# Loading the identity alone, halving the first token tile and the first weight block, and spreading the second gain row earlier in a hybrid encoder trunk

## The chip, the cores and the metric

The kernel runs on one core of a Trainium2 chip. The metric is the device time of one execution in microseconds, as the median of several runs. Smaller is better.

## The reference, cut to what matters

The whole program is one layer of a bidirectional encoder trunk for 512 tokens of width 1024. The change touches only its first few microseconds: the first RMSNorm, and the first product with the input projection.

```
def rmsnorm(x, g):
    y = x32 * rsqrt(mean(x32 * x32, axis=-1) + 1e-6)
    return y * g

proj = rmsnorm(x, norm_mix) @ w_in + b_in     # (512 x 1024) @ (1024 x 4624)
...                                           # two recurrent scans, out projection
x = x + cross_attention(rmsnorm(x, norm_xattn), rmsnorm(mem, norm_mem), ...)
x = x + relu(rmsnorm(x, norm_mlp) @ w_up) ** 2 @ w_down
return rmsnorm(x, norm_final)
```

## The kernel before, in words

The tokens lie in four tiles of 128 rows by 1024 columns (`xtile[0]` to `xtile[3]`, the buffers `as` in the trace). A tile is normalised, multiplied by the gain, turned by TensorE so that the columns lie on the partitions, and split into a high part (fp32r, made by ScalarE) and a low part (the rest, made by VectorE). The weights come in blocks of 128 by 1024 (`st`) that are split in the same way into `wh` and `wl` (`split_out`, L258). A product is then three matmuls: high times high, high times low and low times high (`mm3`, L261 to L263).

The gain row must stand on all 128 partitions. It arrives as one row of 4 KB (`grow1[96:97]`, the buffer `rg`, L149) and TensorE spreads it, 512 columns at a time, by a product with a matrix of ones into PSUM (`spread(0)` and `spread(1)`, L164; the results are `gmix[0]` and `gmix[1]`). `keep_busy` (L160) issues matmuls whose result nobody reads. The constants `cs` (L151) hold the identity that the transposes need (`ident`), two masks and a small selector, 392 columns in all.

For tile 0 the order is written out by hand for TensorE, VectorE and ScalarE, and each of these engines works through its own queue in that order:

- `x_stat(0)`: the sum of squares, half of it on ScalarE (L333), half on VectorE (L335), the two added on VectorE (L336); then GpSimd takes the power -0.5 (L340).
- `x_scale(0, 0)` (L344, VectorE): the left 512 columns times that number and times `gmix[0]`.
- `x_turn(0, 0)` (L349, TensorE): four transposes of 128 columns. Then `spread(1)`.
- `split(0)`: weight block 0 into high and low; `x_split(0, 0)`: the transposes' result into high and low.
- `x_stat(1)` (L338, ScalarE): the sum of squares of tile 1, behind tile 0's split in ScalarE's queue. GpSimd's power, VectorE's `x_scale(1, 0)` and the split of weight block 1 follow it.
- `part_v(0, 0)`: the first six matmuls of the product, tile 0 with weight block 0. Then the transposes of tile 1 and `part_v(0, 1)`, tile 0 with weight block 1, and so on.

The loads go through two queues. SP's queue issues tile 0, weight block 0, tile 1, weight block 1, tiles 2 and 3, and further weight blocks. ScalarE's queue issues the gain row and behind it `cs`.

Of the kernel before, what the change touches and what calls it, by code (L numbers as in the profile page):

```python
# [11 lines left out]
F32R = mybir.dt.float32r  # L12
U8 = mybir.dt.uint8
AF = mybir.ActivationFunctionType
ALU = mybir.AluOpType
# [3 lines left out]
P = 128  # L19
# [20 lines left out]
C_ID, C_MF, C_MB, C_SEL, NC1 = 0, 128, 256, 384, 392  # L40
# [40 lines left out]
def trunk(ctx: ExitStack, tc: tile.TileContext, x, mem, wpk, vec, cst, lmask, rmask, rows, out):  # L81
    nc = tc.nc
# [4 lines left out]
    v, sc, gp, pe = nc.vector, nc.scalar, nc.gpsimd, nc.tensor  # L87
    cnt = [0]

    def nm(s):  # L90
        cnt[0] += 1
        return f"{s}_{cnt[0]}"

    def T(tag, w, bufs, dt=F32):
        return (sb if w == 516 else big).tile([P, w], dt, tag=tag, name=nm(tag), bufs=bufs)

    def mmb():
        return psm.tile([P, 512], F32, tag="mm", name=nm("mm"))

    def smb():  # L100
        return pss.tile([P, 512], F32, tag="sm", name=nm("sm"))

    def tiny(w):
        return sb.tile([P, w], F32, tag=f"tiny{w}", name=nm("tiny"), bufs=2 if w == 8 else 6)

    def ap(t, off, *dims):
        a = t[:, :]
        return bass.AP(a.tensor, a.offset + off, [list(a.ap[0])] + [list(d) for d in dims])
# [12 lines left out]
    cs = sb.tile([P, NC1], F32, name="cs")  # L121
# [3 lines left out]
    ident = cs[:, C_ID:C_ID + P]  # L125
    grow1 = RG()
# [3 lines left out]
    xtile = [z[:, 0:1024] for z in xfull]  # L130
# [10 lines left out]
    def behind(a, b):  # L141

        tc.add_manual_dep(a.ins, b.ins.name, mybir.DependencyInfo(mybir.DependencyClass.NoSync, mybir.DependencyReason.DATA),
                          reason="order of an engine")

    def load_x(t):
        nc.sync.dma_start(out=xtile[t], in_=x[t * P:t * P + P, :])

    row_load = nc.scalar.dma_start(out=grow1[96:97, :], in_=rows[0:1, :])  # L149
    load_x(0)  # L150
    behind(nc.scalar.dma_start(out=cs, in_=cst[:, 0:NC1]), row_load)  # L151
    for g in range(2):
        v.memset(grow1[0:96, g * 512:g * 512 + 512], 0.0)
    gmix = [smb(), smb()]
    idle = mmb()

    def keep_busy(n):

        for _ in range(n):
            pe.matmul(idle[:, 0:P], lhsT=ones[:, 0:P], rhs=ones[:, 0:P], start=True, stop=True)  # L160

    def spread(g):

        pe.matmul(gmix[g], lhsT=ones[0:97, 0:P], rhs=grow1[0:97, g * 512:g * 512 + 512], start=True, stop=True)  # L164

    with tc.manual_schedule(engines={mybir.EngineType.PE}):
        keep_busy(6)
        spread(0)
        keep_busy(4)

    def small_setup():
        lmf = A4()
        nc.sync.dma_start(out=vc, in_=vec)
        nc.sync.dma_start(out=lmf[:, 0:len(LEVELS) * P], in_=lmask)
        for j in range(2):
            a = lmf[64 * j:64 * j + 64, 64 * j:NLV * P]
            v.tensor_copy(lm[64 * j:64 * j + 64, :].rearrange("p (l t) -> p l t", t=64),
                          bass.AP(a.tensor, a.offset, [list(a.ap[0]), [P, NLV], [1, 64]]))
        le, lr = tiny(8), tiny(8)
        lg = vc[:, V_LB:V_LB + 8]  # L180
        v.tensor_tensor(out=le, in0=lg, in1=lg, op=ALU.subtract)
        sc.activation(le, le, AF.Exp)
        v.reciprocal(lr, le)
        v.tensor_tensor(out=le, in0=le, in1=lr, op=ALU.mult)
        v.tensor_tensor(out=lb[:, 0:8], in0=le, in1=le, op=ALU.subtract)
        v.tensor_scalar(out=lb[:, 8:16], in0=lb[:, 0:8], scalar1=-1.0, scalar2=1.0, op0=ALU.mult, op1=ALU.add)
        v.tensor_copy(selr[0:64, :], cs[0:64, C_SEL:C_SEL + 8])
        v.tensor_copy(selr[64:128, :], cs[0:64, C_SEL:C_SEL + 8])
        v.tensor_scalar(out=negb, in0=vc[:, V_FF:V_FF + 8], scalar1=-1.0, scalar2=None, op0=ALU.mult)
# [40 lines left out]
    st_tiles, hl_tiles = {}, {}  # L230

    def load(i):
        if i >= NSTREAM or i in st_tiles:
            return
        t = T("st", 1024, 3)
        nc.sync.dma_start(out=t, in_=wpk[i])
        st_tiles[i] = t

    def split(i):
        if i >= NSTREAM or i in hl_tiles:  # L240
            return
        load(i)
        s = st_tiles[i]
        hi, lo = T("wh", 1024, 3, F32R), T("wl", 1024, 3, F32R)
        made = split_out(hi, lo, s)
        hl_tiles[i] = (hi, lo)
        return made[1]
# [9 lines left out]
    def split_out(dst_hi, dst_lo, src):  # L257
        return sc.activation(dst_hi, src, AF.Copy), v.tensor_tensor(out=dst_lo, in0=src, in1=dst_hi.bitcast(F32), op=ALU.subtract)  # L258
# [56 lines left out]
    xT = XT()  # L315
# [10 lines left out]
    rx, tp = {}, {}  # L326

    def x_stat(t):

        ss = tiny(1)  # L330
        if t == 0:
            s0, s1 = tiny(1), tiny(1)
            sc.activation(junk[:, 512:1025], xfull[t][:, 512:1025], AF.Square, scale=1.0 / 32, accum_out=s1)  # L333
            xg = xfull[t][:, 0:512]
            v.scalar_tensor_tensor(out=junk0[:, 0:512], in0=xg, scalar=1.0 / D, in1=xg, op0=ALU.mult, op1=ALU.mult, accum_out=s0)  # L335
            v.tensor_tensor(out=ss, in0=s0, in1=s1, op=ALU.add)  # L336
        else:
            sc.activation(junk, xfull[t], AF.Square, scale=1.0 / 32, accum_out=ss)  # L338
        rx[t] = tiny(1)
        gp.tensor_tensor(out=rx[t], in0=ss, in1=nh, op=ALU.pow)  # L340

    def x_scale(t, g):
        xg = xtile[t][:, g * 512:g * 512 + 512]
        v.scalar_tensor_tensor(out=xg, in0=xg, scalar=rx[t], in1=gmix[g], op0=ALU.mult, op1=ALU.mult)  # L344

    def x_turn(t, g):
        tp[t, g] = smb()
        for k in range(4):
            pe.transpose(tp[t, g][:, k * P:k * P + P], xtile[t][:, g * 512 + k * P:g * 512 + k * P + P], ident)  # L349

    def x_split(t, g):
        p3 = tp[t, g][:, :].rearrange("p (k t) -> p k t", t=P)
        split_out(ap(xT[g], t * P, [1024, 4], [1, P]), ap(xT[g], 512 + t * P, [1024, 4], [1, P]), p3)

    acc_v = [mmb() for _ in range(4)]

    def part_v(t, q):
        w = hl_tiles[q]  # L360
        for k in range(2):
            kk = 2 * q + k
            z = slice(k * 512, k * 512 + 512)
            mm3(acc_v[t], xs[kk][0][:, t * P:t * P + P], xs[kk][1][:, t * P:t * P + P], w[0][:, z], w[1][:, z], kk == 0, kk == 7)

    ET = mybir.EngineType
    with tc.high_priority(), tc.manual_schedule(engines={ET.PE, ET.DVE, ET.Activation}):
        x_stat(0)
        x_scale(0, 0)
        x_turn(0, 0)  # L370
        spread(1)
        split(0)
        x_split(0, 0)
        x_stat(1)
        part_v(0, 0)
        x_scale(1, 0)
        x_turn(1, 0)
        split(1)
        x_stat(2)
        part_v(0, 1)  # L380
        x_split(1, 0)
        x_scale(2, 0)
        part_v(1, 0)
        x_turn(2, 0)
        x_stat(3)
        x_scale(3, 0)
        part_v(1, 1)
        x_turn(3, 0)
        x_scale(0, 1)
        x_split(2, 0)  # L390
        x_scale(1, 1)
        part_v(2, 0)
        x_split(3, 0)
        x_turn(0, 1)
        split(2)
        part_v(2, 1)
        x_split(0, 1)
        x_turn(1, 1)
        x_scale(2, 1)
        part_v(3, 0)  # L400
        x_split(1, 1)
        x_scale(3, 1)
        part_v(3, 1)
        x_turn(2, 1)
        x_split(2, 1)
        part_v(0, 2)
        x_turn(3, 1)
        x_split(3, 1)
        part_v(1, 2)
        part_v(2, 2)  # L410
        split(3)
        part_v(3, 2)
        small_setup()


# [484 lines left out]
    for t in range(2):  # L900
        a = mt[t]
# [5 lines left out]
        ss = tiny(1)  # L907
# [418 lines left out]
    for f in range(4):  # L1326
# [6 lines left out]
        for p in range(4):  # L1333
            a = []
# [14 lines left out]
            h, l = a11[:, o:o + 256], a11[:, o + 256:o + 512]  # L1349
# [6 lines left out]
            s1, s2, s3, s4 = sa[:, 0:256], sa[:, 256:512], sb_[:, 0:256], sb_[:, 256:512]  # L1356
# [106 lines left out]
```

## Time and profile before

| what | value |
|---|---|
| median of 3 runs | 832.44 us (832.35 to 832.47) |
| time of the profiled execution | 832.41 us |
| its span, first to last instruction | 830.3 us |
| mean granted TensorE clock | 0.998 |
| busy: PE, DVE, ACT, POOL | 818.2, 594.5, 430.0, 77.4 us |

PE is TensorE's matmuls, PEld its weight loads, DVE is VectorE, ACT is ScalarE, POOL is GpSimd, SP is SyncE; ACTq and SPq are the queues from which DMAs are issued. The time lies 2.1 us above the span. PE is busy for nearly the whole span, so what a change in the first microseconds is worth shows as a shift of everything behind it.

### The profile page before, as it was taken

Reading aid. Unit: us, or ns where it says so; the run is one execution under the profiler, and the core shown is the slowest. Engines: PE = TensorE matmul, PEld = TensorE weight load, DVE = VectorE, ACT = ScalarE, POOL = GpSimd, SP = SyncE. Lnnn points to the kernel's source line nnn. Section 1 sums busy time; section 2 is a strip of 40 time slices with the busy share of each in tenths; the row PEclk is TensorE's granted clock in tenths of the full one; section 3 lists DMA queues with packets and bytes.
Section 4 is the critical chain, followed back from the end, with each engine's and each line's share of the span. In section 5 each row is a group of like instructions: output and inputs, shape, how many; then the busy total and the mean of one; then the engine's idle time right before and its main releaser. Section 6 shows DMA issues by size and latency. Waiting matters only on the chain.

```text
span 830.3 us, 11722 instructions
## 1 busy us (share of the span) xinstructions
PE 818.2 (99%) x4414; PEld 681.7 (82%) x4414; DVE 594.5 (72%) x1046; ACT 430.0 (52%) x767; POOL 77.4 (9%) x131
## 2 busy tenths in 40 slices
PE   8999999999999999999999999999999999999996
PEld 6788888887878989887888888888888888888885
DVE  6568875699569988555558985676568666756685
ACT  5247455443678475455546575453444345434544
POOL 2000000100010000100000004012102210220001
PEclk9999999999999999999999999999999999999999
DMA  7332223222342344532352349969836982798332
GB/s 276 117 133 78 77 78 102 79 89 79 117 123 68 123 138 147 151 98 85 118 127 60 84 124 299 264 158 270 238 102 176 274 214 98 185 293 206 109 69 102
DMA packets 34122, 118.86 MB, mean 143 GB/s; under 512 B 3921, under 2 KB 4049, under 8 KB 34066
## 3 DMA queue, kind: packets, MB, share of 16 engines
q1 hardware_dynamic: 22832, 77.80, 27.4%
q0 software_dynamic: 10944, 39.85, 21.7%
q8 instruction: 35, 0.57, 0.3%
q10 hardware_dynamic: 290, 0.47, 0.2%
q14 instruction: 21, 0.17, 0.1%
HBM read 116.00 MB, written 2.10 MB: 142 GB/s over the span
## 4 chain that ended last, share of the span: by engine, by line
PE 89%; issue 5%; DVE 2%; DMA 1%; ACT 1%; POOL 1%; POOLq 0%; ACTq 0%
PE mm L261 18%; PE mm L263 18%; PE mm L262 18%; PE sm L1155 6%; PE sm L1153 6%; PE sm L1154 6%; PE sm L485 2%; PE mm L1155 2%; PE mm L1153 2%; PE mm L1154 2%; PE sm L827 1%; PE sm L562 1%; DVE wl L258 1%; PE sm L263 1%; PE sm L261 1%
## 5 line engine op out<-in xcount | busy, mean ns | idle before, releaser
L258 ACT ACTIVATE wh<-st 128x1024 fp32r<-128x1024 f32 x131 | 138.7, 1060 | 189.8 <-PE mm L262 117.8
L261 PE MATMUL mm<-xT,wh 128*128 128x512 f32 x544 | 215.2, 396 | 0.0
L258 DVE TENSOR_TENSOR wl<-st,wh 128x1024 fp32r<-128x1024 f32 x131 | 160.2, 1224 | 75.5 <-ACT wh L258 75.0
L263 PE MATMUL mm<-xT,wl 128*128 128x512 f32 x544 | 213.0, 392 | 0.1
L262 PE MATMUL mm<-xT,wh 128*128 128x512 f32 x544 | 212.3, 390 | 0.3 <-DVE xT L975 0.3
L263 PEld LDWEIGHTS mm<-xT,wl 128*128 128x128 f32 x544 | 102.1, 188 | 21.7 <-DVE wl L258 0.3
L262 PEld LDWEIGHTS mm<-xT,wh 128*128 128x128 f32 x544 | 102.2, 188 | 21.0 <-DVE xT L975 0.9
L261 PEld LDWEIGHTS mm<-xT,wh 128*128 128x128 f32 x544 | 102.2, 188 | 20.9 <-ACT wh L258 0.3
L1102 POOL DMA_DIRECT2D as<-in_wpk x52 | 39.6, 764 | 250.2 <-DVE wl L258 165.1
L1342 DVE SCALAR_TENSOR_TENSOR t<-mm,rg 128x512 f32<-128x512 f32 x32 | 22.0, 691 | 52.1 <-PE mm L263 52.0
L1153 PE MATMUL sm<-wh,yT 128*128 128x512 f32 x128 | 49.8, 389 | 0.0
L1154 PE MATMUL sm<-wl,yT 128*128 128x512 f32 x128 | 49.8, 389 | 0.0
L1155 PE MATMUL sm<-wh,yT 128*128 128x512 f32 x128 | 49.8, 389 | 0.0
L258 ACT ACTIVATE wh<-as 128x1024 fp32r<-128x1024 f32 x26 | 27.6, 1062 | 37.0 <-PE sm L1155 23.7
L258 DVE TENSOR_TENSOR wl<-as,wh 128x1024 fp32r<-128x1024 f32 x26 | 31.9, 1226 | 14.0 <-ACT wh L258 13.9
L1153 PE MATMUL sm<-wh,a 128*128 128x512 f32 x84 | 32.9, 391 | 0.0
L1155 PE MATMUL sm<-wh,a 128*128 128x512 f32 x84 | 32.7, 389 | 0.0
L1154 PE MATMUL sm<-wl,a 128*128 128x512 f32 x84 | 32.7, 389 | 0.0
L1285 DVE TENSOR_TENSOR vv<-vv,sm 128x512 f32<-128x512 f32 x48 | 31.0, 681 | 1.7 <-PE sm L1155 1.7
L199 POOL TENSOR_TENSOR tiny<-tiny,misc 128x4 f32<-128x4 f32 (+1 forms) x10 | 9.6, 963 | 204.6 <-DVE tiny L197 139.5
L1154 PEld LDWEIGHTS sm<-wl,yT 128*128 128x128 f32 x128 | 24.0, 188 | 5.0
L1155 PEld LDWEIGHTS sm<-wh,yT 128*128 128x128 f32 x128 | 24.0, 188 | 5.0
(329 smaller groups left out, 1581.1 us busy)
## 6 DMA issues: line engine op xcount, KB each, us to landing
st<-in_wpk SPq DMA_DIRECT2D x131, 512.0 KB, 3.4
as<-in_wpk POOLq DMA_DIRECT2D x52, 512.0 KB, 7.0
gate<-in_wpk POOLq DMA_DIRECT2D x24, 512.0 KB, 6.9
as<-in_x SPq DMA_DIRECT2D x4, 512.0 KB, 6.7
vv<-in_x SPq DMA_DIRECT2D x8, 256.0 KB, 4.5
out<-vv SPq DMA_DIRECT2D x7, 256.0 KB, 2.2
a<-in_mem SPq DMA_DIRECT2D x2, 512.0 KB, 3.7
t<-in_rows SPq DMA_DIRECT2D x2, 256.0 KB, 4.9
```

What stands on the lines that cost most here:

```text
L199: gp.tensor_tensor(out=r, in0=ms, in1=nh.to_broadcast([P, w]), op=ALU.pow)
L258: return sc.activation(dst_hi, src, AF.Copy), v.tensor_tensor(out=dst_lo, in0=src, in1=dst_hi.bitcast(F32), op=ALU.subtract)
L261: pe.matmul(ps, lhsT=ah, rhs=bh, start=first, stop=False)
L262: pe.matmul(ps, lhsT=ah, rhs=bl, start=False, stop=False)
L263: pe.matmul(ps, lhsT=al, rhs=bh, start=False, stop=last)
L485: mm = pe.matmul(ps[64 * i:64 * i + 64, z:z + 64], lhsT=kc[j][:, w * P + 64 * i:w * P + 64 * i + 64], rhs=rhs(j, w * P, i), start=True, st ...
L1102: return gp.dma_start(out=dst, in_=wpk[idx], **kw)
L1153: pe.matmul(ps, lhsT=ah, rhs=bh, start=new, stop=False, **fl)
L1154: pe.matmul(ps, lhsT=ah, rhs=bl, start=False, stop=False, **fl)
L1155: pe.matmul(ps, lhsT=al, rhs=bh, start=False, stop=end and k == 1, **fl)
L1285: added = v.tensor_tensor(out=z, in0=z, in1=ps, op=ALU.add if sign > 0 else ALU.subtract)
L1342: v.scalar_tensor_tensor(out=y, in0=ps, scalar=0.0, in1=rrow[:, 0:512], op0=ALU.max, op1=ALU.mult)
```

## The change

Five edits, all for the first tile:

1. ScalarE's queue loads the identity first (128 columns instead of the 392 of `cs`) and the gain row behind it. The other 264 columns of `cs` are loaded later by SP's queue, between `vc` and the level masks.
2. `spread(1)` stands directly behind `spread(0)`, ahead of the transposes. Of the four `keep_busy` matmuls behind `spread(0)` one is left.
3. The two halves of tile 0's sum of squares are added by GpSimd instead of VectorE.
4. `x_scale(0, 0)`, `x_turn(0, 0)` and `x_split(0, 0)` are each cut into two pieces of 256 columns (`first_half`, `first_split`).
5. The split of weight block 0 is cut into two pieces of 512 columns (`weight_half`); on each of ScalarE and VectorE the order is weight half 0, tile half 0, weight half 1, tile half 1.

```diff
-    row_load = nc.scalar.dma_start(out=grow1[96:97, :], in_=rows[0:1, :])
+    id_load = nc.scalar.dma_start(out=ident, in_=cst[:, C_ID:C_ID + P])
     load_x(0)
-    behind(nc.scalar.dma_start(out=cs, in_=cst[:, 0:NC1]), row_load)
+    behind(nc.scalar.dma_start(out=grow1[96:97, :], in_=rows[0:1, :]), id_load)
...
         keep_busy(6)
         spread(0)
-        keep_busy(4)
+        spread(1)
+        keep_busy(1)
...
         nc.sync.dma_start(out=vc, in_=vec)
+        nc.sync.dma_start(out=cs[:, P:NC1], in_=cst[:, P:NC1])
...
-            v.tensor_tensor(out=ss, in0=s0, in1=s1, op=ALU.add)
+            gp.tensor_tensor(out=ss, in0=s0, in1=s1, op=ALU.add)
...
+    def first_half(h):
+        z = slice(h * 256, h * 256 + 256)
+        a = xtile[0][:, z]
+        v.scalar_tensor_tensor(out=a, in0=a, scalar=rx[0], in1=gmix[0][:, z], op0=ALU.mult, op1=ALU.mult)
+        tp[h] = smb()
+        for k in range(2):
+            pe.transpose(tp[h][:, k * P:k * P + P], xtile[0][:, h * 256 + k * P:h * 256 + k * P + P], ident)
+
+    def first_split(h):
+        p3 = tp[h][:, 0:256].rearrange("p (k t) -> p k t", t=P)
+        split_out(ap(xT[0], h * 2048, [1024, 2], [1, P]), ap(xT[0], h * 2048 + 512, [1024, 2], [1, P]), p3)
+
+    def weight_half(h):
+        z = slice(h * 512, h * 512 + 512)
+        split_out(hl_tiles[0][0][:, z], hl_tiles[0][1][:, z], st_tiles[0][:, z])
...
+        hl_tiles[0] = T("wh", 1024, 3, F32R), T("wl", 1024, 3, F32R)
         x_stat(0)
-        x_scale(0, 0)
-        x_turn(0, 0)
-        spread(1)
-        split(0)
-        x_split(0, 0)
+        first_half(0)
+        first_half(1)
+        weight_half(0)
+        first_split(0)
+        weight_half(1)
+        first_split(1)
         x_stat(1)
```

On ScalarE the queue began like this before (`rg` is the gain row, `cs` the constants, `as_71` tiles 0 and 1, `wh` and `xT` the high parts of weights and tokens, the last row tile 1's sum of squares):

```order
L149 DMA rg_70<-in_rows 1x1024
L139 ACT_TABLE_LOAD
L139 ACTIVATE misc<-misc 128x1
L151 DMA cs<-in_cst 128x392
L333 ACTIVATE xT_106,tiny_127<-as_71 128x513
L258 ACTIVATE wh_140<-st_107 128x1024
L258 ACTIVATE xT_105<-sm_134 128x4x128
L338 ACTIVATE xT_106,tiny_146<-as_71 128x1025
```

Now ScalarE's queue begins like this:

```order
L149 DMA cs<-in_cst 128x128
L139 ACT_TABLE_LOAD
L139 ACTIVATE misc<-misc 128x1
L151 DMA rg_70<-in_rows 1x1024
L335 ACTIVATE xT_104,tiny_127<-as_71 128x513
L260 ACTIVATE wh_123<-st_105 128x512
L260 ACTIVATE xT_103<-sm_134 128x2x128
L260 ACTIVATE wh_123<-st_105 128x512
L260 ACTIVATE xT_103<-sm_138 128x2x128
L340 ACTIVATE xT_104,tiny_149<-as_71 128x1025
```

The gain row has moved from the first to the second place among the DMAs, and half of the weight block's split from ahead of tile 0's split to its middle.

On TensorE the start of the program was this before (L160 is `keep_busy`, L164 `spread`, L349 the transposes, L261 and on the product):

```order
L160 MATMUL mm_89<-t_4_74 128x128 x6
L164 MATMUL sm_87<-rg_70,t_4_74 128x512
L160 MATMUL mm_89<-t_4_74 128x128 x4
L349 MATMUL sm_134<-cs,as_71 128x128 x4
L164 MATMUL sm_88<-rg_70,t_4_74 128x512
L261 MATMUL mm_119<-wh_140,xT_105 128x512
```

It is now this (L366 is the transposes in `first_half`, L263 the product's first matmul):

```order
L160 MATMUL mm_89<-t_4_74 128x128 x6
L164 MATMUL sm_87<-rg_70,t_4_74 128x512
L164 MATMUL sm_88<-rg_70,t_4_74 128x512
L160 MATMUL mm_89<-t_4_74 128x128
L366 MATMUL sm_134<-cs,as_71 128x128 x2
L366 MATMUL sm_138<-cs,as_71 128x128 x2
L263 MATMUL mm_117<-wh_123,xT_103 128x512
```

The second spread has moved from behind the transposes to ahead of them, so everything on TensorE from the transposes on now stands behind both spreads.

## Rows read from the trace of the kernel before

**Rows 1.** Stretches of 20 us: busy time of each engine, granted clock, DMA
```profile
0.00:20.00 20.00, 17.18 (x81) 13.07 (x82) 12.64 (x19) 11.37 (x18) 4.46 (x21) 1.00 0.75 286
20.00:40.00 20.00, 19.91 (x95) 15.85 (x94) 11.25 (x24) 5.54 (x8) 0.00 (x0) 1.00 0.39 121
```
**Rows 2.** Chain of work, first 12 us: start, duration, what
```profile
1.36 5.42 DMA cs<-in_cst
...
9.29 0.57 POOL tiny L340
...
10.54 1.23 DVE wl L258
11.81 0.50 PE mm L262
```
**Rows 3.** Timeline of TensorE: start, duration, operation, count [idle before]
```profile
1.00 2.93 PE L160 MATMUL mm<-t 128*128 128x128 f32 x12 [1.00 <-POOL as L138]
3.72 1.26 PE L164 MATMUL sm<-rg,t 97*128 97x512 f32 x2
4.82 1.06 PE L160 MATMUL mm<-t 128*128 128x128 f32 x8
6.91 0.63 PE L349 MATMUL sm<-cs,as 128*128 128x128 f32 x4 [1.04 <-DMA cs<-in_cst]
7.38 1.02 PE L164 MATMUL sm<-rg,t 97*128 97x512 f32 x2
```
**Rows 4.** Timeline of ScalarE, 4 to 9 us
```profile
4.42 0.63 ACT L333 ACTIVATE xT<-as 128x513 fp32r<-128x513 f32 x1 [1.62 <-DMA as<-in_x]
4.95 0.19 ACT L333 ACTIVATION_READ_ACCUMULATOR xT<-as 128x1 f32 x1
5.82 1.06 ACT L258 ACTIVATE wh<-st 128x1024 fp32r<-128x1024 f32 x1 [0.68 <-DMA st<-in_wpk]
7.58 0.60 ACT L258 ACTIVATE xT<-sm 128x512 fp32r<-128x512 f32 x1 [0.70 <-PE sm L349]
8.07 1.05 ACT L338 ACTIVATE xT<-as 128x1025 fp32r<-128x1025 f32 x1
```
**Rows 5.** Timeline of VectorE and GpSimd, 5 to 9 us
```profile
5.17 0.16 DVE L336 TENSOR_TENSOR tiny<-tiny,tiny 128x1 f32<-128x1 f32 x1
5.41 0.55 POOL L340 TENSOR_TENSOR tiny<-tiny,misc 128x1 f32<-128x1 f32 x1 [4.30 <-DVE tiny L336]
6.00 0.75 DVE L344 SCALAR_TENSOR_TENSOR as<-as,tiny,sm 128x512 f32<-128x512 f32 x1 [0.67 <-POOL tiny L340]
6.91 1.23 DVE L258 TENSOR_TENSOR wl<-st,wh 128x1024 fp32r<-128x1024 f32 x1 [0.16 <-ACT wh L258]
8.21 0.69 DVE L258 TENSOR_TENSOR xT<-sm,xT 128x512 fp32r<-128x512 f32 x1
```
**Rows 6.** DMA issues: ScalarE's first (ACTq), SP's second (SPq), its time to landing
```profile
0.74 0.53 ACTq L149 DMA_DIRECT2D rg<-in_rows  x1
1.17 0.42 SPq L236 DMA_DIRECT2D st<-in_wpk  x1
st<-in_wpk SPq DMA_DIRECT2D x1, 512.0 KB, 4.6
```
**Rows 7.** DMA queues, stretches from 1.6, 2.0 and 4.2: packets, MB, share
```profile
q10 hardware_dynamic: 2, 0.00, 3.1%
...
q1 hardware_dynamic: 194, 0.73, 95.7%
...
q1 hardware_dynamic: 204, 0.76, 79.1%
q10 hardware_dynamic: 144, 0.20, 23.1%
```
**Rows 8.** DMA packets from 14.75 to 15.0 us, mostly of 468 bytes
```profile
DMA packets 78, 0.08 MB, mean 325 GB/s; under 512 B 64, under 2 KB 64, under 8 KB 78
q1 hardware_dynamic: 78, 0.08, 95.0%
```

## The prediction

> **What bounds the kernel now.** [...]
>
> Next the chain of waits [rows 2], to see what the start waits for. It runs from the constants' DMA (1.36 to 6.78) through the transposes, then ScalarE's sum of squares of tile 1 (8.07, [rows 4]), GpSimd's power (9.29), `x_scale(1, 0)` and the low part of weight block 1 on VectorE (10.54 to 11.77) to the matmul at 11.81. From there on TensorE is fed. **So the time that counts is not the first product of tile 0, but when ScalarE begins tile 1's sum of squares: 8.07.** Tile 0's product begins in the shadow of that chain. In ScalarE's queue that sum stands behind all of tile 0's split, and its row shows no wait of its own: tile 1 had landed.
>
> Last the timelines of tile 0 [rows 3 to 5]. The transposes at 6.91 waited for the constants, which landed at 6.78, but the scaling that they also need ran from 6.00 to 6.75. The two arrive almost together; an earlier identity alone would give 0.1 us.
>
> **The change part by part.** The sum is made for the start of tile 1's sum of squares.
>
> *Gain row behind the identity.* This is the costly edit. Before, the row was ScalarE's first DMA, issued at 0.74 [rows 6], and its two packets moved before 2.0 (the first stretch, 1.6 to 2.0) [rows 7]. Now it takes the place of `cs`, issued at about 1.36 [rows 2]. How was a DMA served that was issued there? From 2.0 to 4.2 the queue q10, which is ScalarE's, moved no packet at all, and SP's q1 moved 194; all 144 of `cs` moved between 4.2 and 6.6 [rows 7]. Weight block 0, issued by SP at 1.17, landed at 1.17 + 4.6 = 5.77 [rows 6], in the middle of that. So the constants were served as if all DMAs stood in one line by time of issue: behind tile 0 and weight block 0. The row is a single data packet on one engine, so its turn comes anywhere in that stretch; I take the middle, 5.4, and the bounds 4.7 (first packets at 4.2, plus the identity's 0.2 below, plus 0.3 for the packet and its signal) and 6.3 (block 0's landing at 5.77 plus the same).
>
> Both spreads wait for it. The spread at 7.38 took 1.02 for two records of 0.59 that start 0.43 apart; its weights lead by about 0.2 [rows 3]. With the row at 5.4, `spread(0)` ends at 5.4 + 0.2 + 1.02 = 6.62.
>
> *`spread(1)` ahead of the transposes.* Two more records (2 x 0.43) and one `keep_busy` (two passes of 1.06 / 8 = 0.13 each) stand ahead of the transposes: 5.4 + 0.2 + 4 x 0.43 + 0.26 = 7.58 instead of 6.91. Before, the second spread cost nothing: it ran from 7.38 to 8.40 while ScalarE split tile 0 from 7.58 [rows 3, 4]. Now its cover is gone.
>
> *Scaling in halves.* A half costs 0.48: 0.75 less a slope of (1.23 - 0.69) / 512 per column times 256 [rows 5]; the bounds are half of 0.75 and all of it. 6.64 to 7.6 for both halves: hidden, since TensorE is free only at 7.58. The transposes end for half 0 at 7.97 (two of the four, some 0.39 of 0.63), for half 1 at 8.21.
>
> *ScalarE's queue.* Its weight half 0 is done early. From the transposes on, one after another: tile half 0, 0.37; weight half 1, 0.60; tile half 1, 0.37. (The 1024 columns took 1.06 and the 512 took 0.60, so 256 less are 0.23 less; an instruction starts some 0.1 before the end of the one ahead, as 8.07 against 7.58 + 0.60 [rows 4].) That is 8.01 to 8.38, to 8.88, to 9.15, and tile 1's sum begins at 9.05. Before, ScalarE did the whole weight block from 5.82 to 6.88, while it had to wait for the transposes anyway, and only one instruction of 0.60 stood between transposes and sum. **Cutting the weight block moves 0.5 us of ScalarE's work from that free time onto the path.**
>
> *Sum: 9.05 - 8.07 = +1.0 us.* The power, `x_scale(1, 0)` and block 1's low part follow unchanged, 12.8 instead of 11.81, and TensorE's feed begins 1.0 later.
>
> *The add on GpSimd.* VectorE's add took 0.16 [rows 5]. No plain add of GpSimd stands in the trace; the bounds are 0.16 and its power on the same shape, 0.55. I take 0.35, 0.2 more than before. It is hidden behind the gain row: the power ends by 6.4 at most with tile 0 0.2 later, and `spread(0)` at 6.62. If the row came early, it would show in full. [...]
>
> *Identity first.* 128 packets of 512 bytes, 8 on each of 16 engines. Small packets took about 0.02 each: 95% of 16 engines in 0.25 us is 3.8 us, less 14 large ones of 0.17 (33.7 us of engine time by 194 in [rows 7]), by 64 [rows 8]. So 0.2 us, which tile 0 may lose if the identity goes first: 0 to 0.2. Later loads gain some 0.4 (`cs` took 23.1% of 16 x 2.4 us, 0.55 an engine [rows 7]), but tile 1 wasn't waited for: no gain. The other 264 columns come behind `vc`, long before the copy into `selr`: nothing.
>
> The profiled execution took 832.41, almost the median of 832.44; so 833.4.
>
> **Rivals.**
>
> *The row comes in time: 832.8.* If the queues take turns, the row follows the identity on its own queue and needn't wait for weight block 0; it lands by 4.5 and both spreads end before the scaling. What speaks for it: the row has only one packet, and was issued within 0.2 us of block 0. Against it: q10's silence from 2.0 to 4.2 [rows 7]. Then the power sets the path. Tile 0 at 4.42 to 4.6, ScalarE's half of the sum done 0.72 later (5.14 to 5.32 [rows 4]), add and hops 0.25 to 0.65, power 0.55: 5.96 to 6.5. First half scaled 0.5 later, its two transposes 0.45, then ScalarE's 0.37 + 0.60 with the overlaps, and the sum of tile 1 begins 1.1 behind the transposes: 8.0 to 8.55, which is -0.1 to +0.5 us, middle +0.35. So even with the row in time there is no gain to speak of, since the halved weight block sits in ScalarE's queue. [...]
>
> *Slow passes at the start: 835, slower.* The first 12 passes of `keep_busy` took 2.93 / 12 = 0.24 each, the eight from 4.82 only 0.13 [rows 3], although the granted clock is given as 1.00 [rows 1]. The pace changed while TensorE was working without a break. Now it has nothing to do from 3.93 until the row lands. If the pace rises late for that, the four spread records start 0.85 apart instead of 0.43, +1.7 us, and the passes of `keep_busy` and the transposes add 0.2: +2.9 in all, 835.3. For it: a pause of 1.5 us where there was none. Against it: nearly all of the work before the change of pace remains. It decides from 1.66 us on (below); in the likeliest case, without it, the row would have to land after 6.05.
>
> *Faster.* It would need tile 1's sum to start before 8.07; all low bounds together give 0.1 us. The work taken away (three `keep_busy`, 0.8 us) lies where TensorE waits.
>
> **How the numbers follow.** The row late at the normal pace 0.52 (+0.3 to +1.9, since every 0.1 of the row's landing is 0.1 of the end), the row in time 0.30, slow passes 0.15, something faster 0.03. The forecast is the likeliest, 833.4. The range 832.3 to 834.7 takes in the second case and the first; it leaves out most of the slow passes and the faster case, under 0.2. A measurement of this kernel can tell about 0.2%, 1.66 us, from no change. The late row beyond 6.05 (0.05) and most of the slow passes (0.13) are slower by that: 0.18; faster 0.03; the same 0.79.
>
> **What the profile will show.** The gain row's DMA lands between 4.7 and 6.3; `spread(0)` begins right behind it, and VectorE's first scaling waits for TensorE, not for GpSimd. The transposes begin at about 7.6, ScalarE's sum of tile 1 at about 9.05, and the last matmul that waits for weight block 1 at about 12.8. Wrong it would be if spreads ran before 5 (the row in time), if their records started more than 0.5 apart (slow passes), or if TensorE's long feed began before 11.8 (a gain that I don't see). If the start is late but the end isn't, some wait behind 12 us had slack that the chain doesn't show.

## The result, and the profile after

The changed kernel takes **835.13 us** in the median of seven runs (833.33 to 836.49), the kernel before 832.44 (832.33 to 832.59, seven runs); the ratio is 1.0032, with an interval of 1.0022 to 1.0042. It is slower, by more than the 0.2% that can be told from no change, and outside the forecast range.

The seven runs fall into two groups by their span: one of 831.0 us and six of 833.0 to 833.3, with no run between. The profiled execution is the one short run, 833.33 us. So this section shows what the change does in the shorter runs; what the longer ones add is shown by the first experiment.

The timeline of TensorE in the changed kernel, to be read against [rows 3]:

```profile
0.99 2.93 PE L160 MATMUL mm<-t 128*128 128x128 f32 x12 [0.99 <-POOL as L138]
4.91 1.96 PE L164 MATMUL sm<-rg,t 97*128 97x512 f32 x4 [0.99 <-DMA rg<-in_rows]
6.70 0.39 PE L160 MATMUL mm<-t 128*128 128x128 f32 x2
6.93 0.83 PE L366 MATMUL sm<-cs,as 128*128 128x128 f32 x4
...
11.13 0.63 PE L351 MATMUL sm<-cs,as 128*128 128x128 f32 x4 [1.31 <-issue]
...
12.22 0.50 PE L264 MATMUL mm<-wl,xT 128*128 128x512 f32 x1 [0.23 <-DVE wl L260]
```

TensorE now stands idle for 0.99 us until the gain row has landed, and runs both spreads (four records, at the usual 0.43 us from one to the next, the first 0.50). The transposes begin at 6.93, where they began at 6.91 before. The matmul that waits for weight block 1 begins at 12.22 instead of 11.81.

ScalarE's timeline in the changed kernel [rows 4]:

```profile
4.73 0.63 ACT L335 ACTIVATE xT<-as 128x513 fp32r<-128x513 f32 x1 [2.05 <-DMA as<-in_x]
...
7.40 0.38 ACT L260 ACTIVATE xT<-sm 128x256 fp32r<-128x256 f32 x1 [0.83 <-PE sm L366]
7.68 0.62 ACT L260 ACTIVATE wh<-st 128x512 fp32r<-128x512 f32 x1
8.20 0.38 ACT L260 ACTIVATE xT<-sm 128x256 fp32r<-128x256 f32 x1
8.46 1.06 ACT L340 ACTIVATE xT<-as 128x1025 fp32r<-128x1025 f32 x1
```

From the first transposed half on, three instructions stand ahead of tile 1's sum of squares, 7.40 to 8.46, 1.06 us; before it was one, 7.58 to 8.07. The sum begins 0.39 later than before.

GpSimd's and VectorE's part [rows 5]:

```profile
5.54 0.19 POOL L338 TENSOR_TENSOR tiny<-tiny,tiny 128x1 f32<-128x1 f32 x1 [4.43 <-ACT xT L335]
5.80 0.55 POOL L342 TENSOR_TENSOR tiny<-tiny,misc 128x1 f32<-128x1 f32 x1
```
```profile
6.39 0.87 DVE L363 SCALAR_TENSOR_TENSOR as<-as,tiny,sm 128x256 f32<-128x256 f32 x2 [1.02 <-POOL tiny L342]
```

VectorE's scaling waits for GpSimd's power here, not for the spread.

The chain of waits, as far as it has the rows that answer to [rows 2], and the DMA queues of the stretch from 2.0 to 4.2 us [rows 7]:

```profile
0.74 0.41 ACTq L149
...
1.25 3.53 DMA rg<-in_rows
...
4.91 1.96 PE sm L164 x4
...
8.58 1.04 ACT xT L340 x2
...
9.69 0.56 POOL tiny L342
...
10.94 1.23 DVE wl L260
```

```profile
q1 hardware_dynamic: 141, 0.52, 62.1%
q10 hardware_dynamic: 139, 0.07, 14.7%
```

The gain row has taken the constants' place at the head of the chain: issued at 1.25, landed at 4.78. The identity's packets now move on q10 in a stretch in which q10 was silent before, and the row's one packet of 4 KB moves behind most of them, at 4.09.

In the short run the wait at 12.22 is 0.41 late and the span is 0.6 longer (830.95 against 830.33). VectorE's last instruction is 0.35 late (826.11 for 825.76); the other 0.27 lies behind it. In the nine profiles with the constants in two loads 4.83 to 4.85 us follow that instruction, in the five with one load 4.55 to 4.57. At the end SP waits for the semaphores of the DMAs one after another; with one DMA more, ScalarE's last store, which was waited for last before (by 829.43), is now waited for first (until 829.62), and all other waits come behind it.

Six runs of seven have 2 us more than that.

### The profile page after: what moved, and what is told of

It is laid out like the page before. It is cut to its first block, busy times and chain, and to the rows that moved or that the text cites. A ratio compares the mean times of both kernels' runs of the same rounds, so it can differ in the third digit from the quotient of the medians.

```text
span 831.0 us, 11715 instructions
## 1 busy us (share of the span) xinstructions
PE 817.7 (98%) x4408; PEld 681.2 (82%) x4408; DVE 594.3 (72%) x1048; ACT 429.8 (52%) x769; POOL 77.8 (9%) x132
## 4 chain that ended last, share of the span: by engine, by line
PE 89%; issue 5%; DVE 2%; ACT 1%; DMA 1%; POOL 1%; POOLq 0%; ACTq 0%
PE mm L263 18%; PE mm L265 18%; PE mm L264 18%; PE sm L1178 6%; PE sm L1177 6%; PE sm L1176 6%; PE sm L508 2%; PE mm L1177 2%; PE mm L1178 2%; PE mm L1176 2%; PE sm L850 1%; PE sm L585 1%; DVE wl L260 1%; PE sm L265 1%; PE sm L264 1%
## 5 line engine op out<-in xcount | busy, mean ns | idle before, releaser
L260 ACT ACTIVATE wh<-st 128x1024 fp32r<-128x1024 f32 (+1 forms) x132 | 138.9, 1053 | 189.8 <-PE mm L264 117.5
L263 PE MATMUL mm<-xT,wh 128*128 128x512 f32 x544 | 215.3, 396 | 0.0
L260 DVE TENSOR_TENSOR wl<-st,wh 128x1024 fp32r<-128x1024 f32 (+1 forms) x132 | 160.2, 1215 | 75.6 <-ACT wh L260 75.0
L263 PEld LDWEIGHTS mm<-xT,wh 128*128 128x128 f32 x544 | 102.2, 188 | 21.0 <-ACT wh L260 0.3
```

Source lines behind the costliest of these rows:

```text
L263: pe.matmul(ps, lhsT=ah, rhs=bh, start=first, stop=False)
```

## The experiments

**What was to be told apart.** Theory A: in the longer runs the row lands as in the short one, but TensorE's passes are still at the slow pace of the first 12 `keep_busy` passes when the spreads run, so that the four records start 0.85 us apart. Theory B: it is the loads, the gain row or another of the start landing some 2 us later in the longer runs.

**The changed kernel again**, without an edit, for a profile of a longer run.

> The changed kernel, not altered, for more times and a second profile. Its first profile is the fastest of seven runs (833.33; span 831.0, the others about 833.1). Theory A (slow passes): TensorE's pause between the first keep_busy matmuls and the gain row lets the first stretch run at the slow pace in most runs. Then there are two groups of spans, about 831.0 and about 833.1, nothing between, and a profile of the slow group has the four spread records about 0.85 us apart instead of 0.43, the transposes near 9 us and the end 2 us later. Theory B (late row): the gain row lands later in most runs than the 4.78 us of the first profile, up to 6.3. Then spans are spread without gaps, and a slow profile has records 0.43 apart that begin near 6.5 us.

Measured: 835.44 us median (832.96 to 836.57, seven runs), ratio 1.0028 (1.0017 to 1.004). Four spans lie at 833.2 to 833.5, three at 830.9 to 831.3. The profiled execution has 833.4. The timelines of TensorE, VectorE and ScalarE, and of the windows view the row of 6 to 8 us (busy time of PE, PEld, DVE, ACT and POOL, then granted clock, DMA share and GB/s):

```profile
4.99 3.75 PE L164 MATMUL sm<-rg,t 97*128 97x512 f32 x4 [1.07 <-DMA rg<-in_rows]
8.53 0.64 PE L160 MATMUL mm<-t 128*128 128x128 f32 x2
8.96 0.90 PE L366 MATMUL sm<-cs,as 128*128 128x128 f32 x4
...
14.45 0.50 PE L264 MATMUL mm<-wl,xT 128*128 128x512 f32 x1 [0.23 <-DVE wl L260]
```
```profile
7.14 0.87 DVE L363 SCALAR_TENSOR_TENSOR as<-as,tiny,sm 128x256 f32<-128x256 f32 x2 [1.68 <-PE sm L164]
```
```profile
10.69 1.06 ACT L340 ACTIVATE xT<-as 128x1025 fp32r<-128x1025 f32 x1
```
```profile
6.00:8.00 2.00, 2.00 (x4) 0.97 (x3) 0.85 (x3) 0.63 (x1) 0.46 (x1) 1.00 1.03 420
```

Theory A holds, B falls. The spreads begin at 4.99, 0.08 after those of the short run, so the row landed as it did there, and tile 0 and weight block 0 are no more than 0.15 later. But the four records take 3.75 us instead of 1.96, and every row behind them is 2.0 to 2.2 late: the transposes at 8.96 (6.93), tile 1's sum at 10.69 (8.46), the last wait at 14.45 (12.22).

The granted clock reads 1.00 in that stretch, as in the short run, but that figure is no measurement there. The trace records the clock only from its first change on, and the view counts the time before as 1.00. The first record, a rise to 1.00, stands at 9.56 us in this run and at 3.92 in the short one, and at 4.19 in the kernel before; in each of the three TensorE's passes and transposes start 0.21 apart before that moment and 0.11 apart after it. So the 1.00 of [rows 1] says nothing of the first 4.19 us either.

**Three more `keep_busy` ahead of the spreads**, so that TensorE doesn't stand idle while the row is on its way.

```diff
-        keep_busy(6)
+        keep_busy(9)
         spread(0)
```

> The changed kernel with nine keep_busy matmuls instead of six ahead of the first spread, so that TensorE works without a break until about the row's landing at 4.8 us. Nothing else is changed, the row still comes second. Theory A: the slow group goes, all runs lie near 833.3 (832.41 + 0.7 to 1.0) and within 0.5 us of each other. Theory B: as slow and as spread as the changed kernel, about 835.

Measured: 833.80 us (833.17 to 835.04, 11 runs), ratio 1.0014 (1.0006 to 1.0023). Nine spans lie at 831.1 to 832.0, so the runs don't agree within the 0.5 us that theory A expected. The group at 833 with a mean granted clock of 0.997 or more is gone, though the row lands as before (the spreads begin at 5.00). Two runs are longer, with spans of 832.9 and 833.2, and in those two the mean granted clock is 0.995. The profiled execution is one of them: TensorE's timeline, and the windows of 12 to 14 and 14 to 16 us:

```profile
5.00 2.22 PE L164 MATMUL sm<-rg,t 97*128 97x512 f32 x4
...
7.28 0.60 PE L366 MATMUL sm<-cs,as 128*128 128x128 f32 x4
...
11.42 0.63 PE L351 MATMUL sm<-cs,as 128*128 128x128 f32 x4 [1.32 <-issue]
...
12.51 0.80 PE L264 MATMUL mm<-wl,xT 128*128 128x512 f32 x1 [0.23 <-DVE wl L260]
13.10 0.63 PE L265 MATMUL mm<-wh,xT 128*128 128x512 f32 x1
13.53 0.63 PE L263 MATMUL mm<-wh,xT 128*128 128x512 f32 x1
```
```profile
12.00:14.00 2.00, 1.77 (x6) 1.20 (x5) 1.74 (x3) 1.63 (x3) 1.00 (x2) 0.61 1.04 358
14.00:16.00 2.00, 2.00 (x7) 1.58 (x6) 1.47 (x3) 0.00 (x0) 1.93 (x8) 0.54 0.95 309
```

This is another loss, at another place: after TensorE had nothing to do for 1.3 us ahead of tile 1's transposes, the granted clock reads 0.61 and 0.54 over these 4 us, and seven matmuls start up to 0.43 apart instead of 0.23: some 1.5 us, about as much as this run is longer than the kernel's short ones (832.9 against 831.1 to 831.4). The runs of the changed kernel have 0.997 to 0.999, so this loss is not theirs. The clock's first rise stands at 5.62 here, during the spreads.

**The same, and four `keep_busy` ahead of tile 1's transposes.**

```diff
+        keep_busy(4)
         x_scale(1, 0)
         x_turn(1, 0)
```

> The changed kernel with nine keep_busy matmuls ahead of the first spread and four more between tile 0's first product and tile 1's transposes, where TensorE otherwise pauses for 1.3 us. The granted clock fell to 0.5 behind that pause in one run with nine. Theory A with the fall: no run shows a granted clock under 1 from 12 to 16 us, the group at 834.8 to 835.0 goes, all runs 833.2 to 833.9. If the fall has nothing to do with the pause, some runs stay near 835.

Measured: 833.34 us (832.80 to 833.96, 11 runs), ratio 1.001 (1.0001 to 1.0019); spans 830.9 to 832.1 in one group, granted clock 0.997 to 0.999 in every run. TensorE's timeline:

```profile
5.00 2.65 PE L164 MATMUL sm<-rg,t 97*128 97x512 f32 x4
...
10.39 1.05 PE L160 MATMUL mm<-t 128*128 128x128 f32 x8
11.86 0.63 PE L351 MATMUL sm<-cs,as 128*128 128x128 f32 x4 [0.42 <-issue]
```

With both pauses filled both kinds of longer run are gone. In this run the four records took 2.65: here too the clock rose only during the spreads, at 6.54, but earlier than the 9.56 of the long run. What is left, 1.0 us against the kernel before, is the late row, ScalarE's order, the 0.27 at the end and, in the profiled run, 0.7 us of slow passes.

**The gain row first, the identity second**, in the changed kernel: no pause at all ahead of the spreads.

```diff
-    id_load = nc.scalar.dma_start(out=ident, in_=cst[:, C_ID:C_ID + P])
+    row_load = nc.scalar.dma_start(out=grow1[96:97, :], in_=rows[0:1, :])
     load_x(0)
-    behind(nc.scalar.dma_start(out=grow1[96:97, :], in_=rows[0:1, :]), id_load)
+    behind(nc.scalar.dma_start(out=ident, in_=cst[:, C_ID:C_ID + P]), row_load)
```

> The changed kernel with the two DMAs of ScalarE's queue exchanged: gain row first, identity second. TensorE then goes from keep_busy to the spreads without a break. Theory A and theory B both expect the time back near before: the power on GpSimd sets the path, tile 1's sum of squares begins near 8.3 us, 832.5 to 832.9, no slow group. If the cost lies in the halves, in GpSimd's add or in the second spread's new place instead (theory C), it stays at 833.3 or above.

Measured: 833.44 us (832.65 to 834.38, 11 runs), ratio 1.0012 (1.0003 to 1.0021); eight spans at 830.8 to 831.5, three at 832.3 to 832.5, those three with a mean granted clock of 0.995. TensorE's timeline of a short run (span 831.3):

```profile
3.72 3.51 PE L164 MATMUL sm<-rg,t 97*128 97x512 f32 x4
...
12.52 0.50 PE L264 MATMUL mm<-wl,xT 128*128 128x512 f32 x1 [0.23 <-DVE wl L260]
```

Theories A and B both expected 832.5 to 832.9; the median lies above, at what theory C expected (833.3 or more). The profile corrects theory A in one point. There is no pause ahead of the spreads here, and yet the four records take 3.51 us, from 3.72 to 7.23; the first clock record, the rise, stands at 6.98. So no pause is needed for slow passes: the pace is slow from the start until the clock rises (passes 0.21 apart, then 0.11), and when that is differs from run to run, from 3.92 to 9.56 in the profiles up to here. The pause still matters. Without one ahead of the spreads the clock had risen by 6.98 in the profiles of three kernels (5.62, 6.54, 6.98), and none of their 33 runs lies with the longer group but for a later fall (the longest without one 832.1); the 9.56 was seen only with the pause. Why a pause should do that, no run here shows.

**Edit 1's order alone**, in the kernel before: identity first, row second, the rest of `cs` later; everything else as before.

```diff
-    behind(nc.scalar.dma_start(out=cs, in_=cst[:, 0:NC1]), row_load)
+    behind(nc.scalar.dma_start(out=grow1[96:97, :], in_=rows[0:1, :]), id_load)
```

> The kernel before with the DMA edit alone: identity first, gain row second, the rest of the constants later; spreads, halves and add as before. Theory A: TensorE has the same pause, so two groups again; at the normal pace about 832.6, at the slow pace the scaling waits for two slow spread records, some 0.8 to 1.2 us more, 833.5 to 834. Theory B: one group, 832.6 to 834 without gaps. Theory C: no change, 832.4.

Measured: 834.49 us (832.58 to 834.59, 11 runs), ratio 1.0018 (1.0009 to 1.0027). Two groups again: three spans at 830.6 to 831.0 and eight at 832.0 to 832.6, whose times (834.00 to 834.59) lie above the 833.5 to 834 expected. The profile shows a short run:

```profile
4.86 1.10 PE L164 MATMUL sm<-rg,t 97*128 97x512 f32 x2 [0.93 <-DMA rg<-in_rows]
5.79 1.06 PE L160 MATMUL mm<-t 128*128 128x128 f32 x8
...
11.91 0.50 PE L263 MATMUL mm<-wl,xT 128*128 128x512 f32 x1 [0.25 <-DVE wl L259]
```

Edit 1 alone gives the longer runs, with only one spread ahead of the transposes: 0.1 us up to the last wait in the profiled short run (11.91 for 11.81), some 2 us in a long one (832.0 to 832.6 for 830.3). The four `keep_busy` are eight passes, and like the spread they stand between the row and the transposes. That no long run was profiled here leaves the slow passes in it argued from the first experiment.

**Edit 2's order alone**, in the kernel before: `spread(1)` behind `spread(0)`, one `keep_busy` instead of four, the row still loaded first.

> The kernel before with edit 2 alone: second spread directly behind the first, one keep_busy matmul behind them, gain row first as before. There is no pause. If the second spread's place costs only where the passes are still slow (the profile of the changed kernel with the row first had four slow records from 3.72 to 7.2), the transposes stand at 6.9 to 7.4 by the run: 832.4 to 832.9, hardly above before. If its place alone costs 2 us, 834.5.

Measured: 832.77 us (832.21 to 834.01, 11 runs), ratio 1.0006 (0.9997 to 1.0015), all spans at 830.2 to 830.8. TensorE's timeline:

```profile
3.71 2.34 PE L164 MATMUL sm<-rg,t 97*128 97x512 f32 x4
5.90 0.39 PE L160 MATMUL mm<-t 128*128 128x128 f32 x2
6.99 0.63 PE L350 MATMUL sm<-cs,as 128*128 128x128 f32 x4 [0.71 <-DMA cs<-in_cst]
```

With the row first, the spreads and the passes behind them end 0.71 us before the transposes, which wait for the constants, although the first two records were slow (2.34 us for the four). Slow passes have that much room here, and 1.04 us in the kernel before [rows 3].

**`spread(1)` behind the transposes**, in the changed kernel, and then **the same with the row first**.

```diff
         spread(0)
-        spread(1)
         keep_busy(1)
...
         first_half(1)
+        spread(1)
         weight_half(0)
```

> The changed kernel with the second spread put back behind the transposes, all else (gain row second, pause, halves, GpSimd's add) as in the change. Theory A (slow passes, and the second spread's place lets them count): at the slow pace two records of 0.85 us fewer stand ahead of the transposes, so the slow group comes from +2.5 down to about +0.7 us, median 833.0 to 833.4. Theory B (the row's landing alone) expects only the two records at the normal pace, 0.86 less, 834.3.

> The changed kernel with the gain row first and the second spread behind the transposes. Nothing slow stands ahead of the transposes any more but the first spread, as before. Theory A: 832.5 to 832.9, one group; what stays above before is the halved weight block in ScalarE's queue and the later tile 0, tile 1's sum of squares at about 8.3. If TensorE's later pause of 1.3 us (10.1 to 11.4) makes the granted clock fall in some runs, those lie 1.6 above.

Measured: 833.84 us (832.84 to 835.32, 11 runs), ratio 1.0017 (1.0008 to 1.0025), with spans from 830.9 to 832.8; and with the row first 832.74 us (832.58 to 833.86, 11 runs), ratio 1.0006 (0.9997 to 1.0015), spans 830.7 to 831.5. Putting the second spread back takes 1.3 us off the median, putting the row back as well the rest of what can be measured. The first of the two medians lies between what theory A (833.0 to 833.4) and theory B (834.3) expected, so it doesn't decide between them.

The profile with the row second (a shorter run, span 830.9) shows which clock the slow pace goes with: the second spread on TensorE's timeline, and the window of 8 to 10 us.

```profile
7.67 1.91 PE L164 MATMUL sm<-rg,t 97*128 97x512 f32 x2
```
```profile
8.00:10.00 2.00, 2.00 (x4) 0.87 (x4) 1.18 (x3) 2.00 (x5) 0.40 (x1) 0.50 1.04 424
```

Behind pauses of 0.89 and 0.70 us the granted clock has fallen to 0.50, and this is recorded. The spread's two records start 0.85 apart, as in the first experiment's long run. The fall made this run no longer: three others without it (mean clock 0.998 for 0.995) have spans of 831.0.

**Edits 4 and 5 alone**, the halves of tile 0 and of weight block 0, in the kernel before.

```diff
...
-        x_scale(0, 0)
-        x_turn(0, 0)
+        first_half(0)
+        first_half(1)
         spread(1)
-        split(0)
-        x_split(0, 0)
+        weight_half(0)
+        first_split(0)
+        weight_half(1)
+        first_split(1)
```

> The kernel before with edits 4 and 5 alone: scaling, transposes and split of tile 0 and the split of weight block 0 in halves; DMAs, spreads and add as before. By the prediction's count tile 1's sum of squares begins 0.2 to 0.5 us later, for half of the weight block sits in ScalarE's queue behind the transposes: 832.6 to 832.9. If the halves let the first product start earlier and that counted, below 832.3.

Measured: 833.00 us (832.61 to 833.30, 11 runs), ratio 1.0008 (0.9999 to 1.0016), spans 830.6 to 831.2. ScalarE's timeline:

```profile
7.47 0.38 ACT L258 ACTIVATE xT<-sm 128x256 fp32r<-128x256 f32 x1 [0.80 <-PE sm L364]
7.75 0.62 ACT L258 ACTIVATE wh<-st 128x512 fp32r<-128x512 f32 x1
8.27 0.38 ACT L258 ACTIVATE xT<-sm 128x256 fp32r<-128x256 f32 x1
8.53 1.06 ACT L338 ACTIVATE xT<-as 128x1025 fp32r<-128x1025 f32 x1
```

Tile 1's sum begins at 8.53, 0.46 late, with no other edit: the same three instructions as in the changed kernel. Of the 0.46, 0.11 is the transposes' own delay in this run (7.02 for 6.91, behind the constants); 0.35 is the halves. The median lies a little above the 832.6 to 832.9 expected, and the interval can't tell it from before.

**Edit 3 alone**, the add on GpSimd, in the kernel before.

> The kernel before with edit 3 alone, the add on GpSimd. The profile of the changed kernel shows the add at 0.19 us and the power 0.34 behind the end of ScalarE's half of the sum, where before it was 0.27. So 0.1 us, hidden in part behind the constants' landing: 832.35 to 832.5, not to be told from before. If GpSimd's add held up more than that, 832.7 or above.

Measured: 832.47 us (832.24 to 833.07, 11 runs), ratio 1.0002 (0.9993 to 1.0011): no difference that can be measured.

**What the parts suggest as a faster kernel**: the row first, the identity alone second, tile 0 in halves, weight block 0 split whole and ahead of their splits, `spread(1)` behind the transposes, four `keep_busy`, the add on VectorE.

> A version that keeps what costs nothing: gain row first, identity alone second, scaling, transposes and split of tile 0 in halves; but the weight block split whole ahead of the tile, the second spread behind the transposes, four keep_busy matmuls behind the first spread and the add on VectorE. ScalarE's tile halves follow the transposes at about 6.95 and 7.4, tile 1's sum of squares begins at about 7.7 instead of 8.07: 832.0, faster than before by 0.3 to 0.5 us. If the sum's start isn't what sets the path, 832.4.

Measured: 832.26 us (832.12 to 833.03, 11 runs) against 832.35, ratio 0.9999 (0.999 to 1.0008). ScalarE's timeline:

```profile
7.01 0.78 ACT L259 ACTIVATE xT<-sm 128x256 fp32r<-128x256 f32 x2 [0.29 <-PE sm L365]
7.94 1.07 ACT L339 ACTIVATE xT<-as 128x1025 fp32r<-128x1025 f32 x1 [0.15 <-DMA as<-in_x]
```

Tile 0's split is done 0.4 us earlier than before, but tile 1's sum gains only 0.13: it now waits for tile 1's own load. VectorE's last instruction begins 0.23 earlier than before (825.53 for 825.76), and the 0.27 behind it, from the constants in two loads, takes that back. No gain that can be measured.

**The kernel before with one `keep_busy` behind `spread(0)` instead of four.**

> The kernel before with one keep_busy in place of the four behind spread(0), and nothing else: the part of edit 2 that has not been run alone. What it is to tell: in the runs so far the time outside the span swings (1.84 to 4.14 us) in just those kernels that issue seven keep_busy in all, and is steady (1.8 to 2.2) in those that issue ten or more, the kernel before among them. Theory K (fewer passes of keep_busy make it swing, wherever the second spread stands): at least two of the eleven runs have over 2.3 us outside the span, the span stays at 830.2 to 830.8, median 832.5 to 832.9. Theory S (it has to do with the place of the second spread or of the gain row): all eleven have 1.8 to 2.2 outside, median 832.3 to 832.6. Beside it the pause: TensorE now has nothing to do from about 5.3 to 6.9 us; if a pause alone made the pace fall, the four transposes and the second spread behind it, 0.63 and 1.02 us before, would take 1.0 and 1.8, and tile 1's sum would begin 0.4 later, at 8.5.

Measured: 832.74 us (832.42 to 833.68, 11 runs), ratio 1.0004 (0.9995 to 1.0013). Two runs have 2.44 and 2.76 us outside the span, nine 1.95 to 2.27; the 15 runs of the kernel before beside them 1.95 to 2.08. That is what theory K expected, except that three spans (830.9, 831.0 and 831.7) lie above its 830.2 to 830.8. TensorE's timeline:

```profile
7.11 0.63 PE L349 MATMUL sm<-cs,as 128*128 128x128 f32 x4 [1.33 <-DMA cs<-in_cst]
7.58 1.02 PE L164 MATMUL sm<-rg,t 97*128 97x512 f32 x2
```

Behind a pause of 1.33 us the transposes and the spread ran at the usual pace: in this run, in which the clock had risen at 5.36, the pause alone slowed nothing.

## Why the prediction was wrong

**The step that failed** is in the third rival: "Against it: nearly all of the work before the change of pace remains", and with it the choice of the usual pace as the likeliest and 0.15 for the slow passes. By their spans ten of the 14 runs of the changed kernel are of that kind; one of the ten was profiled. The rival itself was right in mechanism and near in size: records 0.85 apart, +2.9 us and 835.3 were forecast; the median came out at 835.13, +2.7. Part of that nearness is luck: the late row and ScalarE's order cost 0.4 where the rival counted 1.0, the waits at the end 0.27 that it didn't count, the slow passes about 2.1 where it counted 1.9.

What the runs showed in place of the argument: the work done before doesn't settle when the pace rises. The same twelve passes stand ahead of the pause in both profiles of the changed kernel, and the clock rose at 3.92 in one, before the spreads, and at 9.56 in the other, behind them. It rose at 4.19 in the profile of before and at 4.64 to 6.98, during the spreads, in the profiles of four experiments. A single profile of before could not show that, because there a swing of this size is hidden: one spread and eight passes that nobody reads stand ahead of the transposes, and these wait another 1.04 us for the constants.

**The row late at the usual pace**, the forecast itself, is nearest to the shorter group, and that its profiled run came out at 833.33 where 833.4 was forecast is luck. By the prediction's own signs that run is as much the rival in which the row comes in time: the spreads ran before 5, the scaling waited for GpSimd and not for TensorE, and tile 1's sum began at 8.46 (the rival's 8.0 to 8.55, not 9.05). Its span is longer than before by 0.6, and 0.3 more of its time lies outside the span. The steps:

- *The gain row lands at 5.4.* It landed at 4.78 and 4.86, at the low bound of 4.7, and the spreads ended at 6.87 instead of at 7.32. That the row would come behind other loads was right, and how far behind was too much: its packet moved at 4.09, behind most of the identity's on its own queue, and landed 0.69 later, where 0.3 was allowed for packet and signal, a term that no run shows. The rival in which the row comes in time had 4.5, the author's estimate; the runs lie between the two and nearer to 4.5.
- *The transposes begin at 7.58.* They began at 6.93: nearly all of it is the row's 0.6 us.
- *ScalarE's queue moves 0.5 us onto the path.* Right: 1.06 us from the first half to tile 1's sum, forecast 1.04. From the first transpose to the sum it is 0.35 to 0.37 more than before, with these edits alone and in the short run, since the first half is ready earlier than the whole was. It is nearly all of what the short run loses up to 12.22.
- *Tile 1's sum +1.0.* +0.39, since the row's 0.6 fell away; the wait for block 1's low part followed by +0.41. Of the span's 0.6, 0.35 is there at VectorE's last instruction.
- *The add on GpSimd, 0.35.* 0.19, where VectorE's took 0.16, and alone it makes no difference to the time that can be measured. In the short run it isn't hidden from the scaling, which waits for the power behind it.
- *The other 264 columns: nothing.* No row shows that their load delayed anything in the first 20 us, but as one DMA more they go with the 0.27 at the end. The prediction put the term at nothing and had no row for it.
- *Smaller readings.* Passes start 0.21 and 0.11 apart; the 0.24 and 0.13 are means over rows that include the first start or the last end. The spread began 0.13 behind the landing, not 0.2. The low bound of the power in the second rival adds up to 5.94, not 5.96. Nothing hangs on these.
- *Identity first: tile 0 later by 0 to 0.2.* ScalarE's half of tile 0's sum began 0.31 later, 4.73 for 4.42. It cost little: the spreads and the passes behind them, not the scaling, held the first transposes.

**What makes the 2.7 us**, then: about 0.4 from the late row and ScalarE's order, where 1.0 was forecast, 0.27 from the waits at the end, and about 2 from slow passes (spans of 833.0 to 833.3 for 831.0). Edit 1 alone brings longer runs on, edit 2 alone does not; edit 2 together with edit 1 puts both spreads where nothing hides them.

**What stays open:** what decides when the pace rises in a run, why it came as late as 9.56 only where the pause was, and why the time outside the span swings. In the six kernels that issue seven `keep_busy` in all (the changed one, with two sets of runs, and five experiments) 24 of 69 runs have over 2.2 us outside the span, up to 4.14; in the six experiments with ten or more none of 66. The last experiment was made on that guess and fits it, but it names no cause. It makes little of the changed kernel's 835.13 (2.13 outside the span in that run; 1.95 to 2.13 in the kernel before), but it can move a median: in the first experiment the run of the median, 835.44, is one of the shorter ones (831.3) with 4.14 outside.

## What to carry to other kernels

Work that must be done before the first product belongs where a late start or a slow pass has room; ask of each instruction put ahead of the first transposes what it costs at the pace of the engine's first microseconds, not at the pace of the row in which it stood later (here 0.85 us from one spread record to the next, not 0.43). Don't put the load that TensorE waits for behind another on its queue to make a wait elsewhere 0.1 us shorter: here the row landed at 4.78 and 4.86 instead of before 3.72. And where runs fall into groups, profile a run of each group before explaining the median.

## What was not expected of the hardware

- The pace of TensorE's passes in the first 9 us differs by a factor of two (records of the spread 0.43 and 0.85 apart in two runs of one kernel), and the moment of the change moves by more than 5 us between runs (3.92 and 9.56). The view's granted clock reads 1.00 on both sides of it, because the trace has no record of the clock before its first change; where a fall was recorded (0.50, 8 to 10 us, `spread(1)` behind the transposes), the same records are 0.85 apart.
- Behind 1.3 us without work the granted clock fell in some runs and not in others: to 0.61 and 0.54 in the 4 us from 12 us on in one run, and not at all in the changed kernel's short run behind 1.31 us at the same place. With `spread(1)` behind the transposes 0.89 and 0.70 us without work stood ahead of a fall to 0.50.
- A row of 4 KB issued at 1.25, half a microsecond after the queue's first load, took 3.53 us to land; issued first, at 0.74, it was there before TensorE asked for it at 3.72.
- Three reader-less matmuls fewer in the first 6 us go with a time outside the span that swings by up to 0.8 us (1.95 to 2.76, eleven runs) in a kernel that is otherwise the same (1.95 to 2.08, 15 runs).
